# Last attention mixer: all products from tokens in natural order, the dilated order made in the rotation and by a scratch in DRAM

## The chip, the cores and the metric

One core of a Trainium2 chip runs the whole program. The metric is device time in microseconds (us) of one execution, lower is better. A measurement of this kernel has a median over some runs, here three.

## The reference, cut to what matters

The program is a chain of layers on 512 tokens of 1024 features in float32: two hybrid layers, then a pooling mixer and an attention mixer, each with a SwiGLU behind it. The change concerns the attention mixer alone. It has 16 heads of 64, in three groups:

```
ATTN_PATTERNS = ((128, 1), (512, 4), (2048, 16))     # window, dilation; 6, 5 and 5 heads
q = rope(h @ Wq) / 8;  k = rope(h @ Wk);  v = h @ Wv
o_g, lse_g = dilated_window_attention(q, k, v, window, dilation)   # per group
alpha = softmax over groups of (logsumexp over the group's heads of lse - log(heads))
y = concat(3 * alpha_g * o_g) @ w_out
```

With dilation 1 a token attends to its own block of 128 and the one before. With dilation 4, tokens t = 4 l + r of one residue r attend among themselves; this is what the program calls (r, l) order: four blocks of 128 tokens with one residue each. The third group (dilation 16) is computed in the same four blocks with a mask.

## The kernel before, in words

Activations lie feature-major: `h[k]` is a tile [128 features, 2, 512 tokens], high and low part of the normed activation; a float32 product is three matmuls (high x high, high x low, low x high), `mm3`, lines 216 to 221. Weights come as a stream: `wall` holds chunks of eight tiles [128 x 128] in the order of use; SP loads a chunk (L175), ACT rounds it to a high part (L184), DVE takes the low part (L193), two or three chunks ahead of its use (`prep_to`, called from `take`).

Two product forms exist. `prodF` (one weight tile per feature tile, eight of them, 24 matmuls) has the weights as the loaded (stationary) operand and 512 tokens of `h` as the moving one. `prodT` gives token-major results: the loaded operand is a block of 128 tokens of `h`, the moving one is a strip of weight columns; 8 feature tiles x 4 token blocks x 3 = 96 matmuls, of 384, 384 and 256 columns for `v1`, `v2`, `v3`.

In `attn_mixer` (L1274) heads go in eight pairs j. Pairs 0 to 2 use natural token order, 3 to 7 the (r, l) order (head 11, in pair 5, belongs to the third group). Before the change the (r, l) order is made where TensorE reads `h`: `pview` is `h` with tokens in steps of four (16 bytes), used as the moving operand of the ten `prodF` of queries and keys of pairs 3 to 7, and as the loaded operand (`tpview`) of the `prodT` of `v2` and `v3`. The rotation tables exist in both orders (`cc[0]`, `cc[1]`).

The order of work on TensorE is the order of emission: (0,0), (1,0), (0,1), (1,1) in the boundary, then the loop: query product (0,2), `prodT` of `v1`, key product (1,2), (0,3), (1,3), ... (1,7), then `prodT` of `v2` and of `v3`. Here (0,j) is queries and (1,j) keys of pair j. An evacuation `rot` (L1290) is three DVE operations from PSUM (L1293 to L1295) and a Pool addition (L1296); queries then take two ACT passes (L1303, L1304).

Between products, `pump` lets up to two side threads take one stage each. A thread `pair_gen(j)` has the stages scores and exponentials (L1343, L1346, L1347, L1349), transposes (L1376, copies L1377), and output (L1391, L1392); it may start scores when its keys were set one pump before, and output only when the flag of its values is old ("v1", "v2", "v3"). `alpha_gen` waits for all scores, then has a chain of small DVE and ACT operations with two sets of small matmuls (L1428, L1430) and leaves the weights in `den` (L1462). `drain` pumps with no product in between until a flag is set. After that each pair's output is scaled (L1503), transposed (L1510), split in two parts (L1517, L1518 or the helper `split`, L309, L310), and multiplied by `w_out`.

Of the kernel before, what the change touches and what calls it, by code (L numbers as in the profile page):

```python
# [21 lines left out]
NCH = 488  # L22
# [6 lines left out]
# columns of the packed small parameters  # L29
# [11 lines left out]
# columns of the small constants  # L41
# [8 lines left out]
def _shape_constants():  # L50
    f = np.float32
    i = np.arange(128)
    j = np.arange(512)
    cst = np.zeros((128, NCST), f)
    neg = f(-1e30)
    cst[:, 128:256] = np.where(i[None, :] >= i[:, None], f(0), neg)
    cst[:, 0:128] = cst[:, 256:384] = np.where(i[:, None] >= i[None, :], f(0), neg)
    cst[:, 384:512] = np.where((i[:, None] >= i[None, :]) & (i[:, None] % 4 == i[None, :] % 4), f(0), neg)
    cst[:, 512:640] = (i[:, None] > i[None, :]) & (i[:, None] // 64 == i[None, :] // 64)
    for n in range(2):  # L60
        cst[:, 640 + n] = i // 64 == n
    for r in range(4):
        cst[:, 642 + r] = i // 32 == r
        cst[:, 646 + r] = i % 4 == r
    cst[:, 650] = np.where((i // 32) % 2 == 0, 0.125, 0)
    cst[:, 651] = np.where((i // 32) % 2 == 1, 0.125, 0)
    for g, w in enumerate((2, 4, 8, 16)):
        cst[:, 652 + 16 * g:668 + 16 * g] = (f(w) / np.minimum(np.arange(16) + 1, w).astype(f))[None]
    # retention decays per head: within a block of 128 [key, query], of a query since its block's start, of a key to its block's end
    lg = [math.log1p(-2.0 ** (-5.0 - h)) for h in range(4)]  # L70
    cd = np.zeros((128, 2, 4, 128))
    for h in range(4):
        ok = (i[None, :] // 64) >= (i[:, None] // 64)
        cd[:, 0, h] = np.where(ok, np.exp(np.abs(i[None, :] - i[:, None]) * lg[h]), 0) * 128 ** -0.5
        cd[:, 1, h] = np.exp(i * lg[h])[None]
        cst[:, 716 + h] = np.exp((128 - i) * lg[h]) * 128 ** -0.5
    cd = cd.reshape(128, 1024).astype(f)

    def rope_tab(half, nrow):
        inv = f(10000.0) ** (-np.arange(half, dtype=f) / f(half))  # L80
        ang = (np.arange(512, dtype=f)[None, :] * inv.astype(f)[:, None]).astype(f)
        c, s = np.cos(ang).astype(f), np.sin(ang).astype(f)
        n = nrow // half
        C = np.concatenate([c] * n, 0)
        Sg = np.concatenate([s] * (n // 2) + [-s] * (n // 2), 0)
        return C, Sg

    C, Sg = rope_tab(64, 128)
    cr = np.concatenate([C, Sg], 1)
    half = 32  # L90
    inv = f(1.0) / (f(10000.0) ** (np.arange(0, 64, 2, dtype=f) / f(64)))
    ang = (np.arange(512, dtype=f)[None, :] * inv.astype(f)[:, None]).astype(f)
    c, s = np.cos(ang).astype(f), np.sin(ang).astype(f)
    C = np.concatenate([c] * 4, 0)
    Sg = np.concatenate([s, s, -s, -s], 0)
    perm = (4 * np.arange(128)[None, :] + np.arange(4)[:, None]).reshape(-1)
    cd2 = np.concatenate([C, Sg, C[:, perm], Sg[:, perm]], 1)
    cr2 = np.zeros((128, 8, 128), f)
    for r in range(4):
        for l in range(128):  # L100
            cr2[4 * (l % 32) + r, r, l] = 1
    for ib in range(4):
        for t in range(128):
            cr2[32 * ib + t // 4, 4 + ib, t] = 1
    return dict(cst=cst, cd=cd, cr=cr, cd2=cd2.astype(f), cr2=cr2.reshape(128, 1024))


def emit(tc, A, log, stop=None, dump=None):
# [36 lines left out]
    # ---------------- constants and parameters  # L145
# [18 lines left out]
    # ---------------- the stream of weight tiles  # L164
# [32 lines left out]
    def take(spec):  # L197
        """the next weight tile [128 x 128]; spec = (name, index, first row, column ranges)"""
        i = st["pos"]
        st["pos"] += 1  # L200
        log.append(spec)
        c, o = divmod(i, 8)
        prep_to(c + st["la"])
        h, l = prepped[c]
        for old in [q for q in prepped if q < c - 5]:
            del prepped[old]
        return (h, l, o * 128)
# [15 lines left out]
    # ---------------- side threads  # L223
# [3 lines left out]
    class Flags(dict):  # L227
# [3 lines left out]
        def old(self, *es):  # L231
            """all set, and not since the last pump"""
            return all(e in self and self[e] < tick[0] for e in es)

    def pump(n=2, ada=True):
        """one stage each of up to n side threads, and one of the modulation's"""
# [23 lines left out]
    # ---------------- products  # L260
# [9 lines left out]
    def prodT(name, idx, c0, ncol, view, evac):  # L270
        """token-major product: out[tb] [128 tokens, ncol]; c0: first column, or the column ranges of each tile"""
# [19 lines left out]
    # ---------------- statistics  # L291
    def colsum(out, sq, c0, n):
        """out[:, i] = sum over partitions of columns c0 + 128 i.. of sq"""
# [9 lines left out]
    def bcast(ps, r, n):  # L303
        """columns of r [128 tokens, n] over all partitions: ps[:, token]"""
# [7 lines left out]
    # ---------------- residual, normed activations  # L312
# [27 lines left out]
    def norm_gen(c0, c1, psB, Ac, Bc):  # L340
        """all feature tiles, one a step, each DVE pass behind the next tile's first"""
# [32 lines left out]
    def upd_sq(upd):  # L374
        """x update of a whole tile, its squares added to the running sum"""
# [11 lines left out]
    def boundary(name, idx, nk, k0, xs, upd, norm, cons):  # L387
        """last two m-tiles of a product in token halves, the norm, and the first four tiles of the next product"""
# [15 lines left out]
        def tot(a):  # L404
            """all squares of the half but the last tile's, then with it"""
# [80 lines left out]
    # ---------------- adaptive modulation  # L486
# [68 lines left out]
    # ================= block 1  # L555
    def silu2_evac(dst):
        """twice the silu of a product"""
# [17 lines left out]
    def attention1(l, group1):  # L575
        """group1(cons) runs the norm and the first group of products"""
# [23 lines left out]
        # derived columns  # L600
# [9 lines left out]
        # ---- retention  # L610
# [16 lines left out]
        def attend(po, blocks, vt, hd):  # L627
            """po [dv, 512] += v^T A over key blocks; blocks[jb] = A[jb] [128 keys, 512-128*jb]"""
# [11 lines left out]
        def norm_out(key, hd, po, gcol, sil):  # L640
            """po [tokens, 4 blocks, 128]: gated, normed branch output in hi and lo parts"""
# [58 lines left out]
        # ---- gated linear attention and forget gates  # L700
# [117 lines left out]
        # ---- gates and the branches' products  # L818
# [35 lines left out]
        # ---- forgetting attention  # L854
# [103 lines left out]
        # ---- output product, first four tiles as the mixed tiles come  # L958
# [15 lines left out]
    def ffn(first, up_spec, evac_a, evac_b, down, upd, nxt):  # L974
        """first(cons) runs the norm and the first four tiles; up_spec(which, f, k); evac_a -> temp; evac_b(temp) -> product"""
# [68 lines left out]
    # ---------------- start: modulation, norm and first group, tile by tile  # L1044
    def start_group(cons):
# [27 lines left out]
        def ada_mul(k, nd):  # L1073
            """products of the rows' blocks of shift and scale of feature tile k from the nd-th on, summed on Pool"""
# [11 lines left out]
        def ada_sum(k):  # L1086
            """the other blocks on DVE, a step each, then the whole sum"""
# [9 lines left out]
        def ada_cols(k, fill=iter(())):  # L1097
            """their columns, steps of other sums in between"""
# [14 lines left out]
        def ada_pe(p, k, kks):  # L1113
            """shift and scale of feature tile k as a row"""
# [75 lines left out]
    # ================= block 2  # L1190
# [84 lines left out]
    def attn_mixer(first):  # L1275
# [14 lines left out]
        def rot(ps, j, dst=None):  # L1290
            C, Sg = [cc[0 if j < 3 else 1][:, i] for i in range(2)]
            a, b = t2("ra"), t2("rb")
            V.tensor_tensor(a, ps, C, op=ALU.mult)  # L1293
            V.tensor_tensor(b[0:64], ps[64:128], Sg[64:128], op=ALU.mult)
            V.tensor_tensor(b[64:128], ps[0:64], Sg[0:64], op=ALU.mult)  # L1295
            PL.tensor_tensor(a if dst is None else dst, a, b, op=ALU.add)  # L1296
            return a
# [21 lines left out]
        def scores_exp(j, u):  # L1319
            """scores and their exponentials of one head, [queries, blocks of keys]"""  # L1320
# [31 lines left out]
        def pair_gen(j):  # L1352
            """one pair of heads: scores to unscaled outputs [queries, heads]"""
# [49 lines left out]
        def alpha_gen():  # L1403
            """weights of the three groups per token, times 3 / denominator, left in den"""
# [26 lines left out]
            # ly: all three in (l, r) order, lx: in token order; [128, 3, 4]  # L1431
# [34 lines left out]
        def pview(k, j):  # L1466
            v = lambda i: h[k][:, i].rearrange("p (l r) -> p r l", r=4)
            return v(0), v(1)

# [8 lines left out]
        hp = [pview(k, 0) for k in range(8)]  # L1478
# [4 lines left out]
        tpview = lambda k, tb: (hp[k][0][:, tb], hp[k][1][:, tb])  # L1483
        for which, j in seq[4:]:
            f = (q_evac if which == 0 else k_evac)(j)
            prodF(*W, 0, 8, hs if j < 3 else hp, lambda m, ps: f(ps), c0=qkcols(which, j))
            if (which, j) == (0, 2):
                F.add("go")
                prodT(*W, [cols(2048 + 128 * i) for i in range(3)] + [()], 384, tview, lambda tb, ps: ACT.copy(v1[tb // 2][:, tb % 2, 0:384], ps))
                F.add("v1")  # L1490
        prodT(*W, [cols(2432 + 128 * i) for i in range(3)] + [()], 384, tpview, lambda tb, ps: ACT.copy(v2[tb // 2][:, tb % 2, 0:384], ps))
        F.add("v2")
        prodT(*W, 2816, 256, tpview, lambda tb, ps: ACT.copy(v3[:, tb], ps))
# [121 lines left out]
def _pack(inputs, log):  # L1615
    """the weight tiles in the order of their use, eight to a chunk"""
# [93 lines left out]
```

## Time and profile before

| What | Value |
|---|---|
| Median of 3 runs | 2961.01 us (2960.27 to 2964.32) |
| Profiled execution: span from the first to the last instruction | 2960.5 us |
| TensorE (PE) busy in the span | 2920.0 us, 99% |
| DVE, ACT, POOL busy | 1477.7, 991.8, 442.6 us |
| Start of (0,2), start of the first product with `w_out` | 2304.07, 2533.20 us |
| Chain that ended last: all other engines than PE | 0% |
| End of the last key product (1,7) | 2477.97 us |
| Start of the next product after those of the first four `w_out` columns | 2558.14 us |

The profiled execution has no other time of its own than its span; the median of the runs is 0.5 us above it. PE is matmul, PEld weight load, DVE VectorE, ACT ScalarE, POOL GpSimd, SP the queue that loads weights. Ends of matmuls are modelled, so the distance from start to start of two matmuls tells what one costs. A float32 matmul with a small operand (scores, transposes, outputs) shows as two records.

### The profile page before, as it was taken

The page shows a single profiled execution, that of the slowest core. Times are in us where ns is not written, and L with a number is a line of the kernel's source. Part 1 is how long each engine was busy: PE and PEld are TensorE (multiplying, and loading weights), DVE is VectorE, ACT ScalarE, POOL GpSimd, SP SyncE. Part 2 cuts the span into 40 slices and gives each one's busy share as a digit, 9 for nine tenths or more (in the row PEclk, how much of TensorE's full clock was granted, in tenths as well). Part 3 has the DMA queues.
Part 4 walks back from the last instruction along what each step waited for, and adds up shares of the span by engine and source line. Part 5 has one row for each costly group of instructions (what it writes and reads, how often), then busy time and mean ns, then how long its engine had stood idle before and what let it go on. Part 6 is the DMA issues. An engine that isn't in the chain of part 4 may idle for free. (4 is left out here: it accounts for less than half of the span.)

```text
span 2960.5 us, 35393 instructions
## 1 busy us (share of the span) xinstructions
PE 2920.0 (99%) x14426; PEld 2430.7 (82%) x14426; DVE 1477.7 (50%) x2076; ACT 991.8 (34%) x1510; POOL 442.6 (15%) x301
## 2 busy tenths in 40 slices
PE   7999999999999999999999999999999999999998
PEld 4888878888889888878988889888888757888887
DVE  6867565675445544354543345643334544443233
ACT  4243332332233144333332333432123324333122
POOL 4212010110111222110110112110011100111011
PEclk8999999999999999999999999999999999999999
DMA  7445434444323223223323322322323111322321
GB/s 285 154 152 181 154 114 142 150 143 161 109 90 114 83 85 101 86 72 102 105 86 102 98 93 79 121 79 93 107 86 121 58 37 49 97 88 91 109 86 50
DMA packets 90055, 319.08 MB, mean 108 GB/s; under 512 B 9850, under 2 KB 12060, under 8 KB 89892
## 3 DMA queue, kind: packets, MB, share of 16 engines
q1 hardware_dynamic: 87908, 313.92, 33.1%
q10 hardware_dynamic: 1984, 2.90, 0.3%
q8 instruction: 113, 1.85, 0.3%
q14 instruction: 50, 0.41, 0.0%
HBM read 314.67 MB, written 2.11 MB: 107 GB/s over the span
## 5 line engine op out<-in xcount | busy, mean ns | idle before, releaser
L219 PE MATMUL mm<-h,wh 128*128 128x512 f32 (+1 forms) x2424 | 930.9, 384 | 0.0
L221 PE MATMUL mm<-h,wl 128*128 128x512 f32 (+1 forms) x2424 | 924.8, 381 | 0.3 <-DVE wl L193 0.3
L220 PE MATMUL mm<-h,wh 128*128 128x512 f32 (+1 forms) x2424 | 925.1, 382 | 0.0
L193 DVE TENSOR_TENSOR wl<-w,wh 128x1024 fp32r<-128x1024 f32 x483 | 630.7, 1312 | 50.6 <-ACT wh L184 49.0
L184 ACT CAST wh<-w 128x1024 fp32r<-128x1024 f32 x488 | 502.1, 1046 | 184.6 <-DVE wl L193 76.6
L221 PEld LDWEIGHTS mm<-h,wl 128*128 128x128 f32 x2424 | 459.0, 189 | 97.8 <-issue 20.2
L219 PEld LDWEIGHTS mm<-h,wh 128*128 128x128 f32 x2424 | 459.0, 189 | 94.7 <-issue 18.7
L220 PEld LDWEIGHTS mm<-h,wh 128*128 128x128 f32 x2424 | 459.1, 189 | 93.5 <-issue 17.7
L219 PE MATMUL mm<-y,wh 128*128 128x512 f32 (+1 forms) x704 | 264.6, 376 | 0.0
L220 PE MATMUL mm<-y,wh 128*128 128x512 f32 (+1 forms) x704 | 264.6, 376 | 0.0
L221 PE MATMUL mm<-y,wl 128*128 128x512 f32 (+1 forms) x704 | 264.5, 376 | 0.0
L282 PE MATMUL mm<-wh,h 128*128 128x512 f32 (+3 forms) x480 | 182.4, 380 | 0.5 <-DVE rb L1295 0.5
L284 PE MATMUL mm<-wl,h 128*128 128x512 f32 (+3 forms) x480 | 179.5, 374 | 0.0
L283 PE MATMUL mm<-wh,h 128*128 128x512 f32 (+3 forms) x480 | 179.3, 374 | 0.0
L981 DVE TENSOR_TENSOR g<-g,mm 128x512 f32<-128x512 f32 x44 | 30.3, 688 | 285.2 <-PE mm L221 276.4
L219 PEld LDWEIGHTS mm<-y,wh 128*128 128x128 f32 x704 | 132.5, 188 | 24.2
L220 PEld LDWEIGHTS mm<-y,wh 128*128 128x128 f32 x704 | 132.5, 188 | 24.1
L221 PEld LDWEIGHTS mm<-y,wl 128*128 128x128 f32 x704 | 132.5, 188 | 24.0
L310 POOL TENSOR_TENSOR y<-u,y 128x512 fp32r<-128x512 f32 x44 | 68.2, 1550 | 525.2 <-ACT y L309 515.9
L310 POOL TENSOR_TENSOR y<-g,y 128x512 fp32r<-128x512 f32 x44 | 68.1, 1547 | 522.7 <-ACT y L309 522.7
L523 DVE SCALAR_TENSOR_TENSOR adaacc<-ada,cact,adaacc 128x512 f32<-128x512 f32 x140 | 127.3, 910 | 3.0
L384 POOL TENSOR_TENSOR acc<-acc,sq 128x512 f32<-128x512 f32 x40 | 59.5, 1486 | 460.0 <-ACT sq L383 459.4
(372 smaller groups left out, 3381.3 us busy)
## 6 DMA issues: line engine op xcount, KB each, us to landing
w<-in_wall SPq DMA_DIRECT2D x488, 512.0 KB, 3.6
ada<-in_wada SPq DMA_DIRECT2D x96, 512.0 KB, 3.6
x<-in_xT SPq DMA_DIRECT2D x8, 256.0 KB, 6.3
cB<-scr ACTq DMA_DIRECT2D x8, 256.0 KB, 4.2
cR<-in_cr SPq DMA_DIRECT2D x2, 512.0 KB
cD<-in_cd SPq DMA_DIRECT2D x2, 512.0 KB, 5.7
c<-in_cd SPq DMA_DIRECT2D x2, 512.0 KB
out<-out SPq DMA_DIRECT2D x2, 512.0 KB, 3.1
```

The source lines that it names most:

```text
L184: ACT.copy(his[i], stage[i])
L193: (eng or V).tensor_tensor(l, stage.pop(i), his[i].bitcast(F32), op=ALU.subtract)
L219: PE.matmul(ps, wh, xh, start=start, stop=False)
L220: PE.matmul(ps, wh, xl, start=False, stop=False)
L221: PE.matmul(ps, wl, xh, start=False, stop=stop)
L282: PE.matmul(ps[tb][:, 0:ncol], xh, wh, start=k == 0, stop=False)
L283: PE.matmul(ps[tb][:, 0:ncol], xl, wh, start=False, stop=False)
L284: PE.matmul(ps[tb][:, 0:ncol], xh, wl, start=False, stop=k == 7)
L310: (eng or V).tensor_tensor(hl[:, 1], src, hl[:, 0].bitcast(F32), op=ALU.subtract)
L384: PL.tensor_tensor(sqa["acc"], sqa["acc"], q, op=ALU.add)
L523: V.scalar_tensor_tensor(acc, src, cact[:, kk:kk + 1], acc, op0=ALU.mult, op1=ALU.add)
L981: V.tensor_tensor(s, s, ps, op=ALU.mult)
```

## The change

Queries and keys of all pairs are now multiplied from `h` in natural order. For pairs 3 to 7 `rot` reads PSUM with a step of four elements and writes in (r, l) order. The values come from two `prodT` of 512 columns instead of three of 384, 384 and 256: the first gives `v1` and the first 128 columns of `v2`, the second the rest. What belongs to `v2` and `v3` is copied by ACT to temporary tiles, written to a DRAM scratch [512, 640] by DMAs from the ACT queue (four of 64 KB, four of 256 KB), and read back in (r, l) order by three DMAs of the same queue. The second `prodT` moves from the end of the loop to behind the key product (1,2). The flags "v2" and "v3" are both set after the loop. The stream has 486 chunks instead of 488.

```diff
         def rot(ps, j, dst=None):
             C, Sg = [cc[0 if j < 3 else 1][:, i] for i in range(2)]
             a, b = t2("ra"), t2("rb")
-            V.tensor_tensor(a, ps, C, op=ALU.mult)
-            V.tensor_tensor(b[0:64], ps[64:128], Sg[64:128], op=ALU.mult)
-            V.tensor_tensor(b[64:128], ps[0:64], Sg[0:64], op=ALU.mult)
+            if j < 3:
+                v = lambda t: t
+            else:
+                v = lambda t: t.rearrange("p (r l) -> p r l", r=4)
+                ps = ps.rearrange("p (l r) -> p r l", r=4)
+            V.tensor_tensor(v(a), ps, v(C), op=ALU.mult)
+            V.tensor_tensor(v(b[0:64]), ps[64:128], v(Sg[64:128]), op=ALU.mult)
+            V.tensor_tensor(v(b[64:128]), ps[0:64], v(Sg[0:64]), op=ALU.mult)
             PL.tensor_tensor(a if dst is None else dst, a, b, op=ALU.add)
...
+        scr2 = dr.tile([S, 640], F32, name="scr2")
+        vperm = scr2.rearrange("(l r) c -> l r c", r=4)
+        def v_evac(tb, ps):
+            ACT.copy(v1[tb // 2][:, tb % 2, 0:384], ps[:, 0:384])
+            t = t2("vs")
+            ACT.copy(t[:, 0:128], ps[:, 384:512])
+            nc.scalar.dma_start(scr2[tb * 128:(tb + 1) * 128, 0:128], t[:, 0:128])
+        def w_evac(tb, ps):
+            t = t2("vs")
+            ACT.copy(t, ps)
+            nc.scalar.dma_start(scr2[tb * 128:(tb + 1) * 128, 128:640], t)
         for which, j in seq[4:]:
             f = (q_evac if which == 0 else k_evac)(j)
-            prodF(*W, 0, 8, hs if j < 3 else hp, lambda m, ps: f(ps), c0=qkcols(which, j))
+            prodF(*W, 0, 8, hs, lambda m, ps: f(ps), c0=qkcols(which, j))
             if (which, j) == (0, 2):
                 F.add("go")
-                prodT(*W, [cols(2048 + 128 * i) for i in range(3)] + [()], 384, tview, lambda tb, ps: ACT.copy(v1[tb // 2][:, tb % 2, 0:384], ps))
+                prodT(*W, 2048, 512, tview, v_evac)
                 F.add("v1")
-        prodT(*W, [cols(2432 + 128 * i) for i in range(3)] + [()], 384, tpview, lambda tb, ps: ACT.copy(v2[tb // 2][:, tb % 2, 0:384], ps))
+            if (which, j) == (1, 2):
+                prodT(*W, 2560, 512, tview, w_evac)
+                for i in range(2):
+                    nc.scalar.dma_start(v2[i][:, :, 0:384], vperm[:, 2 * i:2 * i + 2, 0:384])
+                nc.scalar.dma_start(v3, vperm[:, :, 384:640])
         F.add("v2")
-        prodT(*W, 2816, 256, tpview, lambda tb, ps: ACT.copy(v3[:, tb], ps))
         F.add("v3")
```

## Rows read from the trace of the kernel before

**Rows 1.** Page of the profile, busy time of each engine.
```profile
PE 2920.0 (99%) x14426; PEld 2430.7 (82%) x14426; DVE 1477.7 (50%) x2076; ACT 991.8 (34%) x1510; POOL 442.6 (15%) x301
```

**Rows 2.** Timeline, PE, product (0,2), natural order: start us, us, engine, line, operation.
```profile
2306.13 0.39 PE L219 MATMUL mm<-h,wh 128*128 128x512 f32 x1
2306.36 0.39 PE L220 MATMUL mm<-h,wh 128*128 128x512 f32 x1
```

**Rows 3.** Timeline, PE: start of product (1,4), and of what follows its 24 matmuls.
```profile
2387.08 0.70 PE L219 MATMUL mm<-h,wh 128*128 128x512 f32 x1
...
2398.21 0.84 PE L1328 MATMUL sd<-k,q 128*128 128x128 f32 x4
```

**Rows 4.** Timeline, PE, the token-major products of `v1`, then of `v3`.
```profile
2313.10 0.33 PE L283 MATMUL mm<-wh,h 128*128 128x384 f32 x1
2313.27 0.33 PE L284 MATMUL mm<-wl,h 128*128 128x384 f32 x1
...
2515.05 0.40 PE L282 MATMUL mm<-wh,h 128*128 128x256 f32 x1
2515.29 0.40 PE L283 MATMUL mm<-wh,h 128*128 128x256 f32 x1
```

**Rows 5.** Groups of weight loads in 2309 to 2334, then 2492 to 2530: busy us, mean ns.
```profile
L283 PEld LDWEIGHTS mm<-wh,h 128*128 128x128 f32 x32 | 6.0, 188 | 0.1
...
L283 PEld LDWEIGHTS mm<-wh,h 128*128 128x128 f32 x48 | 15.8, 330 | 0.0
```

**Rows 6.** Timeline, all engines, last key product's rotation and the last pair's scores.
```profile
2478.19 0.69 DVE L1293 TENSOR_TENSOR ra<-mm,c 128x512 f32<-128x512 f32 x1 [6.80 <-PE mm L221]
2480.42 1.29 POOL L1296 TENSOR_TENSOR k<-ra,rb 128x512 f32<-128x512 f32 x1 [11.47 <-DVE rb L1295]
2484.53 1.95 PE L1343 MATMUL sd<-k,q 128*128 128x128 f32 x16
2485.69 0.69 DVE L1346 TENSOR_TENSOR e<-sd,cst 128x512 f32<-128x512 f32 x1 [2.90 <-PE sd L1343]
2487.14 0.41 ACT L1349 ACTIVATE e<-e,nmx 128x128 f32<-128x128 f32 x1 [6.54 <-DVE nmx L1347]
2490.25 1.03 ACT L184 CAST wh<-w 128x1024 fp32r<-128x1024 f32 x1
```

**Rows 7.** Three source lines: ns min/median/max; L1518 writes and reads in steps of four elements.
```profile
L309 ACT CAST o<-sd x3: 592/594/608, 2532.6 to 2538.9; 128x512 fp32r<-128x512 f32 x3
...
L1518 DVE TENSOR_TENSOR o<-sd,o x5: 1085/1091/1096, 2546.8 to 2559.6; 128x512 fp32r<-128x512 f32 x5
...
L310 DVE TENSOR_TENSOR o<-sd,o x3: 684/691/693, 2533.2 to 2539.6; 128x512 fp32r<-128x512 f32 x3
```

**Rows 8.** Timeline, the weights of the groups (`alpha_gen`), then one pair's output.
```profile
2493.66 1.28 ACT L1409 ACT_TABLE_LOAD   x1
2499.93 0.31 DVE L1423 TENSOR_SCALAR lg<-lg 128x4 f32<-128x4 f32 x3
2504.12 0.95 PE L1428 MATMUL sd<-lg,pm 128*128 128x4 f32 x8
2506.53 0.16 DVE L1444 TENSOR_SCALAR lx<-lg 128x4 f32<-128x4 f32 x1
2507.74 0.16 DVE L1451 TENSOR_REDUCE m<-lx 128x4 f32<-128x12 f32 x1
2511.01 0.36 DVE L1462 TENSOR_TENSOR den<-den,q 128x24 f32<-128x24 f32 x3
2536.53 1.89 PE L1391 MATMUL sd<-v,pt 128*128 128x64 f32 x16
```

**Rows 9.** Timeline, ACT queue in layer 0: a DRAM scratch written, then read by four DMAs.
```profile
228.67 0.53 ACTq L740 DMA_DIRECT2D scr<-fp  x1
230.11 1.90 ACTq L742 DMA_DIRECT2D cB<-scr  x4
```

**Rows 10.** Windows: us, busy of PE, PEld, DVE, ACT, POOL, granted clock, DMA share, GB/s.
```profile
1866.00:1870.00 4.00, 4.00 (x13) 3.12 (x13) 2.50 (x6) 1.31 (x2) 0.00 (x0) 0.65 0.19 20
```

More of the change, by code (lines that the diff above doesn't have):

```diff
@@ L21 @@
 EPS = 1e-6
-NCH = 488
+NCH = 486
 LA, LD = 2, 1
@@ L1464, in alpha_gen @@
             yield
-        def pview(k, j):
-            v = lambda i: h[k][:, i].rearrange("p (l r) -> p r l", r=4)
-            return v(0), v(1)
         seq = []
@@ L1477, in attn_mixer @@
         hs = hx()
-        hp = [pview(k, 0) for k in range(8)]
         v1 = [g4("v1", shape=(128, 2, 512)) for _ in range(2)]
@@ L1482, in attn_mixer @@
         tview = lambda k, tb: (h[k][:, 0, tb * 128:(tb + 1) * 128], h[k][:, 1, tb * 128:(tb + 1) * 128])
-        tpview = lambda k, tb: (hp[k][0][:, tb], hp[k][1][:, tb])
+        scr2 = dr.tile([S, 640], F32, name="scr2")
[9 more added lines that the diff above has]
+            nc.scalar.dma_start(scr2[tb * 128:(tb + 1) * 128, 128:640], t)
         for which, j in seq[4:]:
             f = (q_evac if which == 0 else k_evac)(j)
-            prodF(*W, 0, 8, hs if j < 3 else hp, lambda m, ps: f(ps), c0=qkcols(which, j))
+            prodF(*W, 0, 8, hs, lambda m, ps: f(ps), c0=qkcols(which, j))
             if (which, j) == (0, 2):
                 F.add("go")
-                prodT(*W, [cols(2048 + 128 * i) for i in range(3)] + [()], 384, tview, lambda tb, ps: ACT.copy(v1[tb // 2][:, tb % 2, 0:384], ps))
+                prodT(*W, 2048, 512, tview, v_evac)
                 F.add("v1")
-        prodT(*W, [cols(2432 + 128 * i) for i in range(3)] + [()], 384, tpview, lambda tb, ps: ACT.copy(v2[tb // 2][:, tb % 2, 0:384], ps))
+            if (which, j) == (1, 2):
[3 more added lines that the diff above has]
+                nc.scalar.dma_start(v3, vperm[:, :, 384:640])
         F.add("v2")
-        prodT(*W, 2816, 256, tpview, lambda tb, ps: ACT.copy(v3[:, tb], ps))
         F.add("v3")
```

## The prediction

> **What bounds the kernel now.** I read the page's busy times first: TensorE is busy for 99% of the span [rows 1], and the chain of waits names no other engine. So time can only come from TensorE's own work in the stretch that is changed, and can be lost there only where TensorE is made to wait. That stretch is (0,2) to the first product with `w_out`, 2304.07 to 2533.20, 229 us. In its timeline I looked at the distance from start to start of two matmuls. With tokens in natural order 512 columns cost 0.23 us [rows 2]; I use 0.227, the 24 of a product 5.45 us. In the ten products of pairs 3 to 7, whose moving operand is read in steps of 16 bytes, 24 matmuls take 11.13 us [rows 3], 0.464 each, with nothing else on TensorE between. In the token-major products 384 columns cost 0.173 for `v1`, but 0.233 for `v2` and also for `v3`, which has only 256 columns [rows 4]. There the loaded operand is read in steps: the weight load takes 330 ns instead of 188 [rows 5], and the load, not the columns, sets the pace.
>
> **The change part by part**, against the span of 2960.5 us.
>
> *Ten products become contiguous.* 10 x (11.13 - 5.45) = -56.8 us.
>
> *Values.* Before, the three products took 17.7 us (`v1`, with 1.1 us of stalls; the work is 96 x 0.173), 22.9 and 22.5 (about 96 x 0.233 each), together 63.1. After, 2 x 96 x 0.227 = 43.6: -19.5 us. Two weight chunks fewer to prepare lie beside TensorE: nothing.
>
> *Side work on TensorE* (scores, transposes, outputs) is the same and stays on the path: 0. What changes is how well it is covered, since the products between are half as long.
>
> *The rotation reads PSUM in steps of four.* No row shows that. Low end: no dearer, 0.69 us an operation [rows 6]. Nearest row: a DVE operation from PSUM with an SBUF output and one input in steps of four, 1.09 against 0.69 [rows 7]. High end: twice 0.69, 1.38, as a moving operand in steps doubled on TensorE [rows 2, 3]. I take 1.09, from the same engine. DVE is idle over half of the span [rows 1], so the price comes only through latency, as follows.
>
> *Stalls before transposes.* Let t = 0 be the end of product (0,j+1), when scores of pair j start. DVE first has the rotation of these queries: from 0.22 (2477.97 to 2478.19, [rows 6]) for 3 x 1.1 to 3.55. Then two additions and two reductions of 0.69 each; the first maximum is there at 4.95. ACT is in order: the queries' two passes of 0.72 come first (Pool's addition takes 1.3, so they end at 6.45), then eight exponentials in 3.1 us (2487.14 to 2490.25, [rows 6]): 9.6. TensorE has done scores (1.7 from their start to what follows, here and below) and product (1,j+1) (5.45) at 7.15, transposes the first head and waits for the second's exponentials: it ends at 10.05 instead of 7.95, a stall of 2.1 us. Before, the product of 11.13 covered this. For pairs 3, 4, 5: +6.3 (0.9 each, 2.7, at the low end; 2.9 each, 8.7, at the high end). Pair 6 falls into the next part. Scores themselves do not wait: keys are ready at 5 us, the product in between is 5.45 and transposes 0.8.
>
> *The tail.* Before, the products of `v2` and `v3` lay behind (1,7) and covered the last pair's scores and the whole chain of `alpha_gen`. After, nothing is left but side work. From the end of (1,7), t = 0: pair 6's transposes end at 2.9; keys of pair 7 are ready at 0.22 + 3.3 + 1.3 = 5.0 (with the wait for Pool); scores start; their exponentials end 5.7 later (2484.53 to 2490.25, [rows 6]), 10.8. The outputs of pairs 3 to 6 fill TensorE from 6.7 to 13.7 (1.73 each, [rows 8]); each one's copy waits on ACT behind those exponentials, then pair 7's transposes and copies follow, to 15.2. Only then comes the first table load of `alpha_gen` on ACT: its first part takes 6.6 us (2493.66 to 2500.24), the second 2.6 (2504.12 to 2506.69), the third 3.6 (2507.74 to 2511.37) [rows 8]: 28.1. Scaling, transposes and the first half of the split (0.69 and 0.59, [rows 7], with 0.4 of matmuls and hand-overs) bring the first `w_out` product to 30.0. TensorE's own work in it (transposes twice 0.8, scores 1.7, five outputs 8.65, the small matmuls 1.7, transposes for `w_out` 0.7) is 14.4; idle 15.6, of which 0.5 were there before: +15.1. Low end, with a rotation of 2.1: 14; high end 16.5.
>
> *Scratch.* ACT gets eight copies more or other, eleven DMA issues of about 0.45 (four in 1.90, [rows 9]), and the reads wait for the last write to land: 1.4 us between write and read in the earlier scratch [rows 9], of 8 KB only. Behind the waiting read on ACT stand the next weight cast, pair 2's last copy and queries (0,3). The second product's copies and issues end at 4.3 us, pair 2's exponentials at 6.4, the reads are issued by 8 to 10, and nothing of that is needed by TensorE before 13 (pair 2's outputs, after (1,3)); casts run three chunks ahead. Price 0, and 5 us if the write takes 10 us to land. Readers of `v2` and `v3` come 90 us later. The first product's evacuation delays pair 0's and 1's exponentials by 2 us: +0.5. SP's queue sees only the faster use of chunks, the pace that the feed-forward layers have all along.
>
> *Clock.* Behind a pause of TensorE in the pooling mixer the granted clock was 0.65 of full over 4 us [rows 10], 2.8 us at the lower of its two levels (1.2 GHz), which lost 1.4 us of work. The change makes new pauses, about 5 us twice in the tail and 2 us before each pair's transposes. I count three or four such dips, +5 us; bounds 0 and 10.
>
> Sum: -56.8 - 19.5 + 6.3 + 15.1 + 0.5 + 5 = -49.4. 2960.5 - 49.4 = 2911.1 for the span, and 0.5 more for the median: 2911.6.
>
> **Rivals.**
> *A, steps in PSUM cost nothing and the clock stays up:* -56.8 - 19.5 + 2.7 + 14 + 0.5 = -59, 2902. For it: PSUM is not SBUF, where the rows show the price. Against: DVE paid 0.4 us more for such steps.
> *B, the rotation costs twice:* stalls 8.7, tail 16.5, clock 8: -42.6, 2918. The Trainium skill bears on this (PSUM - Partial Sum Buffer, Specifications): it gives PSUM lines of 8 bytes and says that any non-contiguous access slows matmuls significantly; for DVE's reads it gives no figure and no run here shows one.
> *C, the products stay at 11.13 us, as steps are not what makes them slow:* only the values are won, -19.5, and the tail lost, +15 and clock +2: 2959. For it: the modelled ends say nothing of a cause. Against: (0,2) and (1,4) differ in the view of `h` alone, and the loads show the same [rows 2, 3, 5]. The Trainium skill (SBUF - State Buffer, "Door 1: The DMA port swizzle") would speak for C: it says that four float32 are a step that one can take for free. The trace disagrees: exactly that step takes 0.464 instead of 0.227.
> *D, slower than before:* DVE becomes the bound of pairs 3 to 7. Per pair it has six rotation operations of X, 2.4 us of weight preparation and 3.4 of scores and copies, 6X + 5.9; before, a pair took 24.8 us of TensorE. Values and tail together are about even, so it decides at 6X + 5.9 > 24.8: X = 3.2 us, 4.6 times the contiguous one. At X = 3.5 it is 5 x 2.1 and a tail longer by 3 x 2.8: some 2975. Against: the dearest step in these rows is 2.05 times.
>
> **How the numbers follow.** The forecast, 2911.6, with its terms between their bounds: 0.60. A 0.17, B 0.13, C 0.03, D 0.02, and 0.05 for a stall that I did not see, above 2926 (the write that lands late, or chunks that come late). The range 2896 to 2926 takes in A and B with some room and leaves about 0.2 outside. About 0.2% is what a measurement of this kernel can tell from no change, 6 us: faster 0.95, same 0.03, slower 0.02.
>
> **What would show it.** Right: matmuls of pairs 3 to 7 at 0.227 us; 192 instead of 288 token-major ones, all at 0.227; between the end of (1,7) and the first `w_out` product about 30 us with TensorE half idle; L1376 waiting some 2 us for exponentials; rotation operations of pairs 3 to 7 at 1.09 us, the term that I know least. Wrong: a wait of TensorE on weights (L193) or of ACT on the scratch's reads over 5 us, a tail far from 30 us, or products of pairs 3 to 7 over 6 us.

## The result and the profile after

The changed kernel takes 2905.95 us, median of 4 runs (2904.25 to 2915.56), against 2962.49 for the kernel before in the same comparison: ratio 0.9817, 95% interval 0.9801 to 0.9832. Forecast were 2911.6 us and a range of 2896 to 2926. The profiled execution has a span of 2904.6 us, 55.9 less than before; the stretch from the start of (0,2) to the last 24 matmuls of the first four `w_out` columns (2303.84 to 2502.20, against 2304.07 to 2558.14) is shorter by 55.7 of them, so next to nothing happened elsewhere. The table of the kernel before calls 2558.14 the start of the product behind those columns; in the trace it is the start of these 24 matmuls. The longest of the four runs, 2915.56 us, is the one with the lowest mean granted clock, 0.989 against 0.993 and 0.994.

The page's busy row, which answers to [rows 1]; TensorE has 68 us less to do:

```profile
PE 2852.1 (98%) x14330; PEld 2402.7 (83%) x14330; DVE 1477.6 (51%) x2074; ACT 989.9 (34%) x1508; POOL 442.0 (15%) x301
```

The timeline of TensorE, changed kernel: two neighbouring matmuls of the second token-major product (they answer to [rows 4]), then the start of query product (0,6) and of what follows it (to [rows 3]). 24 matmuls now take 5.58 us instead of 11.13, and the token-major matmuls of 512 columns are 0.23 us apart:

```profile
2366.89 0.39 PE L283 MATMUL mm<-wh,h 128*128 128x512 f32 x1
2367.12 0.40 PE L284 MATMUL mm<-wl,h 128*128 128x512 f32 x1
...
2421.92 0.49 PE L219 MATMUL mm<-h,wh 128*128 128x512 f32 x1
...
2427.50 0.38 PE L1349 MATMUL sd<-k,q 128*128 128x128 f32 x2
```

The first operation of the rotation by its source line, ns min/median/max. Six of the 16 read PSUM contiguously and ten in steps of four, and all take the same. So the step has no price here; I had taken 1.09 us from [rows 7]:

```profile
L1299 DVE TENSOR_TENSOR ra<-mm,c x16: 684/692/692, 2303.0 to 2449.0; 128x512 f32<-128x512 f32 x16
```

The timeline of all engines from the end of (0,7) to the first `w_out` product; (1,7) ends at 2448.76. The chain to follow: rotation, exponentials (to the weight cast at 2449.77), transposes that wait a moment for them, then scores of pair 7 that wait for the keys, the table load on ACT, the small matmuls, the group weights, the transposes for `w_out`. It answers to [rows 6, 8]:

```profile
2441.78 0.69 DVE L1299 TENSOR_TENSOR ra<-mm,c 128x512 f32<-128x512 f32 x1 [2.22 <-PE mm L221]
2446.68 0.39 ACT L1355 ACTIVATE e<-e,nmx 128x128 f32<-128x128 f32 x1
2449.77 1.03 ACT L184 CAST wh<-w 128x1024 fp32r<-128x1024 f32 x1
...
2448.76 1.48 PE L1382 MATMUL sd<-ident,e 128*128 128x128 f32 x8
2452.89 2.05 PE L1349 MATMUL sd<-k,q 128*128 128x128 f32 x16 [2.65 <-POOL k L1302]
...
2463.55 1.28 ACT L1415 ACT_TABLE_LOAD   x1
2470.09 1.84 PE L1434 MATMUL sd<-lg,pm 128*128 128x4 f32 x8 [4.77 <-issue]
2477.69 0.36 DVE L1468 TENSOR_TENSOR den<-den,q 128x24 f32<-128x24 f32 x3
2478.82 1.94 PE L1528 MATMUL sd<-ident,os 128*128 128x128 f32 x8 [5.17 <-DVE os L1521]
2480.58 0.80 PE L219 MATMUL mm<-o,wh 128*128 128x512 f32 x1
```

From the end of (1,7) to the first `w_out` product 31.8 us pass, which I call the tail; forecast were 30.0 and something for the clock. The waits of TensorE's matmuls from 2380 to 2500 (us in total, times, longest) are these four and no others:

```profile
PE sd L1528 <- DVE os L1521: 5.2, 1, 5.2
PE sd L1434 <- issue: 4.8, 1, 4.8
PE sd L1349 <- POOL k L1302: 2.6, 1, 2.6
PE sd L1397 <- DVE pt L1383: 0.4, 1, 0.4
```

Windows of the tail, with busy times of PE, PEld, DVE, ACT, POOL, then granted clock, DMA share and GB/s (they answer to [rows 10]). The clock goes to its lower level, 1.2 GHz, at 2468.3 and stays there for 17.1 us; the small matmuls are 0.21 us apart instead of 0.11, and the first 12 `w_out` matmuls take 5.2 us instead of 3.3:

```profile
2460.00:2468.00 8.00, 4.88 (x43) 4.54 (x41) 1.85 (x8) 4.77 (x7) 0.00 (x0) 1.00 0.34 118
2468.00:2480.60 12.60, 5.33 (x25) 5.08 (x25) 5.96 (x33) 4.32 (x8) 0.00 (x0) 0.51 0.04 8
2480.60:2485.80 5.20, 5.20 (x14) 3.76 (x14) 3.58 (x5) 1.53 (x2) 0.00 (x0) 0.55 0.26 93
```

The scratch, by the DMA view (KB each, median us to landing). The first read is issued at 2384.58, 5.1 us behind the last write's issue, and ACT was idle for 3.43 us before the weight cast behind the reads; TensorE waits for nothing there. It answers to [rows 9]:

```profile
v<-scr ACTq DMA_DIRECT2D x1, 512.0 KB, 6.3
...
scr<-vs ACTq DMA_DIRECT2D x4, 256.0 KB, 2.0
```

### The profile page after: what moved, and what is told of

Read it like the earlier page. It is cut to its first block, busy times and chain, and to the rows that moved or that the text cites. A ratio compares the mean times of both kernels' runs of the same rounds, so it can differ in the third digit from the quotient of the medians.

```text
span 2904.6 us, 35206 instructions
## 1 busy us (share of the span) xinstructions
PE 2852.1 (98%) x14330; PEld 2402.7 (83%) x14330; DVE 1477.6 (51%) x2074; ACT 989.9 (34%) x1508; POOL 442.0 (15%) x301
## 4 chain that ended last, share of the span: by engine, by line
PE 94%; DVE 3%; ACT 1%; issue 1%; POOL 1%; DMA 0%; SPq 0%; DVEq 0%; POOLq 0%; ACTq 0%
PE mm L219 25%; PE mm L220 25%; PE mm L221 25%; PE mm L282 3%; PE mm L284 3%; PE mm L283 3%; PE sd L219 1%; PE sd L220 1%; PE sd L221 1%; PE sd L630 1%; PE sd L904 1%; PE sd L296 0%; POOL rs L301 0%; DVE wl L193 0%; DVE ab L1092 0%
## 5 line engine op out<-in xcount | busy, mean ns | idle before, releaser
L219 PE MATMUL mm<-h,wh 128*128 128x512 f32 (+1 forms) x2424 | 909.5, 375 | 0.0
L220 PE MATMUL mm<-h,wh 128*128 128x512 f32 (+1 forms) x2424 | 903.5, 373 | 0.0
L221 PE MATMUL mm<-h,wl 128*128 128x512 f32 (+1 forms) x2424 | 902.9, 372 | 0.3 <-DVE wl L193 0.3
L282 PE MATMUL mm<-wh,h 128*128 128x512 f32 (+1 forms) x448 | 171.1, 382 | 0.1
L284 PE MATMUL mm<-wl,h 128*128 128x512 f32 (+1 forms) x448 | 168.2, 375 | 0.0
L283 PE MATMUL mm<-wh,h 128*128 128x512 f32 (+1 forms) x448 | 168.1, 375 | 0.0
```

What stands on the lines that cost most here:

```text
L219: PE.matmul(ps, wh, xh, start=start, stop=False)
L220: PE.matmul(ps, wh, xl, start=False, stop=False)
L221: PE.matmul(ps, wl, xh, start=False, stop=stop)
L282: PE.matmul(ps[tb][:, 0:ncol], xh, wh, start=k == 0, stop=False)
L283: PE.matmul(ps[tb][:, 0:ncol], xl, wh, start=False, stop=False)
L284: PE.matmul(ps[tb][:, 0:ncol], xh, wl, start=False, stop=k == 7)
```

## The experiments

| Kernel | us, median | Ratio to before, 95% |
|---|---|---|
| the change | 2905.95 | 0.9817 (0.9801 to 0.9832) |
| the change, measured again (`e10`) | 2908.65 | 0.9821 (0.9807 to 0.9834) |
| rotation alone (`e1`) | 2907.36 | 0.9814 (0.9799 to 0.9829) |
| values alone (`e2`) | 2969.46 | 1.0019 (1.0009 to 1.0029) |
| values alone, pauses filled (`e9`) | 2958.91 | 0.9987 (0.9978 to 0.9996) |
| the change, pauses filled (`e7`) | 2903.37 | 0.9802 (0.9788 to 0.9816) |
| the change, group weights' thread first (`e6`) | 2909.18 | 0.9825 (0.9811 to 0.9839) |
| the change, second values product last (`e4`) | 2896.37 | 0.9776 (0.9761 to 0.9790) |
| `e4` with the scratch read by SP (`e8`) | 2891.16 | 0.9761 (0.9747 to 0.9774) |
| before, in steps of two (`e5`) | 2942.38, one run | - |

The theory: the ten contiguous products give 56 us; what the values give, 18 us, is lost again in the tail that their products used to cover, part of it by the clock. The rivals: the values have a gain of their own; the tail is bound by DVE and ACT alone; the scratch's round trip is the price.

**e1, the rotation alone.** The values as before:

```diff
-                prodT(*W, 2048, 512, tview, v_evac)
+                prodT(*W, [cols(2048 + 128 * i) for i in range(3)] + [()], 384, tview, ...)
...
+        prodT(*W, [cols(2432 + 128 * i) for i in range(3)] + [()], 384, tpview, ...)   # behind the loop
+        prodT(*W, 2816, 256, tpview, lambda tb, ps: ACT.copy(v3[:, tb], ps))
```

> Half of the change alone: the ten query and key products of pairs 3 to 7 read h in natural order and the rotation permutes; the values are as before (three token-major products, those of v2 and v3 at the end of the loop, from tokens in steps). My theory: the products give -55.7 us and two things hang on the values alone, -18.3 us of work and the uncovered tail, +17 and +2 for the clock, which cancel. So 2962.5 - 55.7 + 1.5 of stalls before transposes = 2908 us, as fast as the whole change (2906); no pause over 1 us between (1,7) and the first w_out product, and the granted clock stays up there. Rival: the values carry a gain of their own and the tail's pause was there anyway: then 2925 us.

2907.36 us, as forecast, and not to be told from the whole change. All that TensorE waited for from 2420 to 2485 was half a microsecond:

```profile
PE mm L219 <- ACT o L309: 0.3, 1, 0.3
PE mm L220 <- DVE o L310: 0.2, 1, 0.2
```

The granted clock was at its lower level for 3.4 us some 28 us behind the end of (1,7), and in the kernel before for as long 29 us behind it. So the whole gain is the rotation's, and the tail's pauses come from the moved values.

**e2, the values alone.** The products of pairs 3 to 7 take `h` in steps again, and the rotation is as before:

```diff
...
-            prodF(*W, 0, 8, hs, lambda m, ps: f(ps), c0=qkcols(which, j))
+            prodF(*W, 0, 8, hs if j < 3 else hp, lambda m, ps: f(ps), c0=qkcols(which, j))
```

> The other half alone: values by two contiguous token-major products and the DRAM scratch, the second one behind (1,2); the products of pairs 3 to 7 read h in steps as before, the rotation is as before. My theory: -18.3 us for the products of the values, +17 in the tail and +2 for the clock there: 2963 us, the same as before (2962.5), with L1376 not waiting for exponentials and the first w_out product 31 to 32 us behind the end of (1,7). Rival: the scratch and the moved product are worth their 18 us, the tail is a matter of the shorter products: 2944 us.

2969.46 us: dearer than I expected, a miss of 6 us on the side of my theory. The tail takes 40.9 us (2501.94 to 2542.79) instead of 31.8. Its windows show what differs: the clock goes down at 2504.8, in the first pause, and stays down for 41 us, so that outputs and transposes run at the lower level too:

```profile
2501.90:2510.00 8.10, 5.01 (x28) 4.73 (x26) 4.22 (x7) 0.87 (x2) 1.26 (x1) 0.68 0.01 3
2510.00:2530.00 20.00, 18.77 (x87) 18.21 (x87) 3.14 (x10) 8.76 (x24) 0.00 (x0) 0.50 0.08 28
2530.00:2542.80 12.80, 5.33 (x25) 5.07 (x25) 5.93 (x33) 4.52 (x9) 0.00 (x0) 0.50 0.15 44
```

**e7, the change with filled pauses.**

```diff
+        def fill(n):
+            d = mmb()
+            for i in range(n):
+                PE.matmul(d, h[i % 8][:, 0, 0:128], h[i % 8][:, 0], start=i == 0, stop=i == n - 1)
...
+        fill(10)      # behind the loop, ahead of the drain; fill(18) ahead of py, px; fill(20) behind them
```

> The whole change, with matmuls of no use in the three pauses of the tail (10 while the last keys are rotated, 18 ahead of the small matmuls, 20 behind them; 512 columns each into a spare PSUM tile, 11 us in all). It takes no wait away and adds work. My theory, the fall of the granted clock costs 4 us of the tail: the clock stays up, the small matmuls go from 0.213 to 0.112 us, the first w_out product from 5.2 to 3.3 us, time 2906 - 4 = 2902. Rival: the tail is bound by DVE and ACT alone and the clock costs nothing: 2906, or more where the useless matmuls run into the useful ones.

2903.37 us. In the trace the tail is 29.8 us instead of 31.8 and the first 12 `w_out` matmuls take 3.4 instead of 5.2, 3.9 us together: the forecast size. The whole trace is only 2.5 us shorter, because (1,7) ends 1.5 us later in it (2450.22 instead of 2448.76). By the medians the gain is 2.6 and 5.3 us against the two measurements of the change. Their eight runs reach from 2904.25 to 2915.56 us, those of this kernel from 2903.12 to 2903.88, under all of them, though the intervals of the ratios overlap. Work of no use made the kernel faster, so the clock, and not only DVE and ACT, is part of the tail. The window of the tail:

```profile
2460.00:2480.00 20.00, 18.38 (x119) 15.58 (x118) 7.80 (x41) 10.38 (x19) 0.00 (x0) 1.00 0.15 54
```

**e9, the values alone with filled pauses, and e10.** The three `fill` of e7 in the kernel of e2; and the changed kernel once more.

> e2_values_only with the useless matmuls of e7_filled_pauses in the same three pauses. e2 came out at 2969.5, 7.5 us over the kernel before, where I had 2963; its granted clock was down from the first pause of the tail on, for 41 us, and the tail took 40.9 us instead of 31.8. My theory, the excess is the clock and nothing of the scratch or the products: with the clock held up the tail is the 29.8 us of e7, the first w_out product takes 3.4 us, and the time is 2962 - 18.3 + 15.4 - 0.5 = 2958. Rival: the excess lies elsewhere (longer products, the scratch), and the time stays above 2964.

> The changed kernel as it is, on the same chip and in the same rounds as e9: 2906 us, against which e7's 2903.4 and e8's 2891.2 are to be read. If a part of their lead were the chip's, this would come out near 2903.

2958.91 us, where 2958 were expected: with the clock up the tail takes 29.8 us (2505.24 to 2535.01), the values alone are worth 4 us, and e2's excess was the clock; the intervals of e2 and e9 lie apart. The scratch and the longer products are in both kernels, so they are not behind it. Two of e2's own ten runs say the same: with a mean granted clock of 0.994 and 0.992 they took 2959.49 and 2963.17 us, while the other eight, at 0.989 and 0.990, took 2967.7 to 2970.6. e10 gave 2908.65. It ran on the chip of e9, while e7 and e8 ran on another; the kernel before took 2962.76 us on the first and 2961.56 on the second, so some 1.2 us of the leads of e7 and e8 over e10 (5.3 and 17.5 us) may be the chip's, and the rest is the kernels'. The window of e9:

```profile
2501.00:2533.00 32.00, 30.18 (x186) 24.75 (x184) 12.03 (x47) 13.90 (x33) 1.27 (x1) 1.00 0.13 41
```

**e6, the group weights' thread first.** In the change its first table load stands on ACT behind the copies of four outputs and of pair 7's transposes; here the thread comes first and yields between its parts:

```diff
-        side.extend(pair_gen(j) for j in range(8))
         side.append(alpha_gen())
+        side.extend(pair_gen(j) for j in range(8))
...
+            yield
             ACT.activation(tmp, tmp, AF.Exp)
...
+            yield
             lg = c16("lg")
...
+            yield
             yield
             yield
             py, px = sdb(), sdb()
```

> The whole change, but the thread of the groups' weights stands ahead of the pairs and yields between its three ACT parts, so that its first table load comes right behind the last pair's exponentials instead of behind the copies of four outputs and of pair 7's transposes; work and products are the same. My theory, ACT's order is a link of the tail: the first table load 4 to 5 us earlier against the end of (1,7), the first w_out product at 28 us behind it instead of 31.8, time 2906 - 4 = 2902. Rival: the copies come late instead, outputs of pairs 5 and 6 wait for PSUM, and the time stays at 2906.

2909.18 us, no gain: the rival's time held, and its reason is a part of it. The table load did come 4.7 us earlier (10.1 us behind the end of (1,7) at 2448.91, instead of 14.8), and the small matmuls 3.3 us. But outputs and transposes now waited for copies on ACT, as the waits of TensorE show:

```profile
PE sd L1382 <- ACT oT L1398: 0.9, 1, 0.9
PE sd L1397 <- ACT oT L1398: 0.6, 1, 0.6
```

The rest of the lead was given back behind the small matmuls: the last output ran behind them, at the lower clock (it fell at 2461.6, 6.7 us earlier), its copy stood in front of the next table load on ACT, and the exponentials behind that load came no earlier than in the change. Timeline of ACT; the first row is the early load, the others the place where the lead was lost:

```profile
2458.96 1.28 ACT L1415 ACT_TABLE_LOAD   x1
...
2473.86 0.58 ACT L1398 COPY oT<-sd 128x512 f32<-128x512 f32 x1 [6.13 <-PE sd L1397]
2474.47 1.28 ACT L1462 ACT_TABLE_LOAD   x1
```

**e4 and e8, the second values product last.** e4 moves it behind (1,7), with side threads in it; the first three pairs' `w_out` products cover the scratch. e8 lets SP issue the reads, right behind the product:

```diff
...
-            if (which, j) == (1, 2):
-                prodT(*W, 2560, 512, tview, w_evac)
...
+        prodT(*W, 2560, 512, tview, w_evac, at=(1, 3, 5, 6))   # pumps behind these k, and one ahead of the evacuation
...
-        for j in range(8):
+        for j in range(3): scale_o(j)
+        for j in range(3): trans_o(j)
+        for i in range(2):
+            nc.scalar.dma_start(v2[i][:, :, 0:384], vperm[:, 2 * i:2 * i + 2, 0:384])   # e8: nc.sync, behind prodT
+        nc.scalar.dma_start(v3, vperm[:, :, 384:640])
+        F.add("v2")
+        F.add("v3")
+        wo(0, range(4))
+        wo(1, range(4))
+        scale_o(3)
+        scale_o(4)
+        trans_o(3)
+        wo(2, range(4))
+        for j in range(3, 8):
...
```

> The whole change, but the second product of the values comes last, behind (1,7), with side threads at four places in it, so that it covers the last pair's scores, transposes and the weights of the groups; the reads of the scratch follow, and the w_out products of pairs 0 to 2 cover them. My theory: the pause of the tail and the fall of the clock go: -15 us, 2892 us, first w_out product some 32 us behind (1,7) with the 22 us product in it, granted clock up, and a pause of some 5 us left where ACT evacuates before the first split. Rival: the round trip through DRAM becomes the new wait in front of the outputs of pairs 3 and 4 (over 8 us), and the time stays at 2902 to 2906.

> As e4_values_last, but the three reads of the scratch are issued by SP right behind the product's evacuation instead of by ACT behind the splits. In e4 ACT stood 4.6 us in front of these reads with a weight cast behind it, and the outputs of pair 3 waited 1.8 us for them, after which the clock fell. My theory: reads land 3 us earlier, no wait for them, no fall of the clock at that place: 2896 - 4 = 2892. Rival: SP's weight chunks now stand behind the reads and come late, 2896 or more.

e4: 2896.37 us, 10 to 12 us under the change where 15 were expected. Of the tail's 13 us of pauses 2.3 are left, in front of the first transposes for `w_out`. But ACT stood idle in front of the reads and the outputs of pair 3 waited for them, as the rival had it, with a smaller price, and the clock, which was to stay up, fell behind these waits. Waits of e4, ACT's and TensorE's, and the window with the fall:

```profile
ACT wh L184 <- issue: 4.6, 1, 4.6
...
PE sd L1399 <- DMA v<-scr: 1.8, 2, 1.1
...
2467.30:2478.30 11.00, 10.22 (x48) 9.33 (x49) 3.64 (x4) 3.12 (x4) 0.00 (x0) 0.69 0.35 105
```

e8: 2891.16 us, the time as forecast. TensorE does not wait for SP's chunks or for the reads, and at the outputs of pair 3 the clock stays up. It did fall elsewhere, for 3.4 us from 2459.2 on, behind the 2.3 us in which TensorE waits for ACT; behind the same pause of 2.3 us in e4 it did not fall. It is the fastest version, 2.4% under the kernel before and 0.5 to 0.6% under the change. What TensorE still waits for in it, from 2420 to 2500, and the window with the fall:

```profile
PE sd L1527 <- ACT vs L1498: 2.3, 1, 2.3
PE mm L219 <- ACT o L311: 0.2, 1, 0.2
...
2457.50:2466.80 9.30, 9.07 (x37) 6.81 (x38) 4.11 (x6) 3.13 (x6) 0.00 (x0) 0.82 0.73 247
```

**e5, the kernel before in steps of two.**

```diff
-            v = lambda i: h[k][:, i].rearrange("p (l r) -> p r l", r=4)
+            v = lambda i: h[k][:, i].rearrange("p (l r) -> p r l", r=2)
...
-        tpview = lambda k, tb: (hp[k][0][:, tb], hp[k][1][:, tb])
+        tpview = lambda k, tb: tuple(hp[k][i][:, tb // 2, tb % 2 * 128:tb % 2 * 128 + 128] for i in range(2))
```

> The kernel before, but where it reads h in steps of four elements (16 bytes) it reads it in steps of two (8 bytes), for the moving operand of the ten products and for the loaded one of v2 and v3; it leaves out the (r, l) order, so its tokens are mixed up in pairs 3 to 7. Question: what makes a step dear? Theory 1, two values per 16 bytes are enough for full speed: 0.227 us per matmul, loads at 188 ns, time 2962.5 - 56 - 16 = 2890 us. Theory 2, any step costs the same: 0.464 and 330 ns, 2962 us. Theory 3, the price grows with the bytes passed over: about 0.34 us and 260 ns, 2930 us.

2942.38 us, a single run, and no theory alone holds. The moving operand costs nearly the same at 8 bytes as at 16: 0.452 and 0.464 us a matmul. The loaded one does not: 195 ns instead of 330, and the 256-column matmuls take 0.12 us instead of 0.233, so it was the load that had set their pace. The products of `v2` and `v3` take 28.6 us instead of 45.4, which with some 2.9 us for the ten products (240 matmuls) makes up the 19.6 us gained. Timeline of TensorE in a query product and in the product of `v3`:

```profile
2446.40 0.63 PE L219 MATMUL mm<-h,wh 128*128 128x512 f32 x1
2446.85 0.63 PE L220 MATMUL mm<-h,wh 128*128 128x512 f32 x1
...
2500.05 0.28 PE L282 MATMUL mm<-wh,h 128*128 128x256 f32 x1
2500.17 0.28 PE L283 MATMUL mm<-wh,h 128*128 128x256 f32 x1
```

and a group of its weight loads (busy us, mean ns), to be set beside [rows 5]:

```profile
L283 PEld LDWEIGHTS mm<-wh,h 128*128 128x128 f32 x64 | 12.5, 195 | 0.0
```

## Why the prediction was right, and which terms were off

| Step | Forecast, us | Measured, us | From |
|---|---|---|---|
| ten products contiguous | -56.8 | -55.7 | 24 matmuls take 5.54 to 5.68 with the hand-over; all ten products 55.7 against 111.4 |
| values' products | -19.5 | -18.3 | 44.8 against 63.1 |
| stalls before transposes | +6.3 | +1.1 | transposes of pairs 3 to 5 take 1.16 to 1.19 instead of 0.80 |
| tail without the clock | +15.1 | +14.9 | e7: 29.8, less TensorE's own work as forecast (14.4) and 0.5 of before |
| clock | +5 | +3.9 | change against e7: tail 2.1, first `w_out` product 1.8 |
| evacuation of the first product | +0.5 | -0.9 | the scores of the first two heads in the first values product take 3.24 instead of 4.15 |
| sum | -49.4 | -55.0 | span: -55.9 |

The mechanism was right and so was each sign but the smallest. The mis-sized term is the stall before the transposes: forecast 2.1 us a pair, measured 0.38. It failed first with its premise, the price of a DVE operation that reads PSUM in steps, for which I took 1.09 us from an operation that writes and reads SBUF in steps; it is 0.69. With that the eight exponentials end 8.3 us behind the scores' start (2441.51 to 2449.77) and not 9.6. The low bound of the same working had the price right and still gave 0.9 a pair. The rest is a second step: I let all four transposes of the second head wait for its last exponential. In the trace of the changed kernel the transposes run as the exponentials come, and only one weight load of a pair's eight waits for one, 0.25 us. Timeline of TensorE (PE) and its weight loads (PEld), pair 5:

```profile
2434.74 1.43 PE L1382 MATMUL sd<-ident,e 128*128 128x128 f32 x8
2435.84 0.14 PEld L1382 LDWEIGHTS sd<-ident,e 128*128 128x128 f32 x1 [0.25 <-ACT e L1355]
2435.93 0.49 PE L219 MATMUL mm<-h,wh 128*128 128x512 f32 x1
```

Of the 6.5 us between forecast and span the stalls make 5.2. The evacuation (1.4), the clock (1.1) and the tail (0.2) go the same way, the misses of the two groups of products (1.1 and 1.2) the other; 0.9 us are not put down to anything.

Two terms came out nearer than their working, which is luck. For the clock I counted three or four dips of 1.4 us, some of them before the transposes of single pairs; there was one fall, of 17.1 us, and none before the tail. For the tail I used the dear rotation: the scores of pair 7 start 4.1 us behind (1,7) instead of 5.0 and their exponentials end at 9.9 instead of 10.8, but by the table load only 0.4 us of this is left (14.8 instead of 15.2).

Rival A had the rotation right; its time of 2902 was too low because the clock did fall, and with the clock held up e7 takes 2903.4. The first measurement, 2905.95, lies nearer to A than to the forecast, the second, 2908.65, nearer to the forecast. Rival B's doubled rotation did not happen: DVE's reads take 692 ns in both forms. The rule of the Trainium skill on PSUM's lines (PSUM - Partial Sum Buffer, Specifications) speaks of matmuls, and this trace shows that it does not carry over to these reads. Rival C, in which steps are not what makes the products slow, fell at once: the matmuls are 0.23 us apart. Rival D never came near its deciding point of 3.2 us.

What I did not see beforehand is how little the second half of the change brings. The sum had it (-19.5 against +15.1 and +5), but the text did not say that the two halves could be had apart. e1 and e2 show that the rotation alone gives the whole gain and that the values alone lose; e9 shows that they win 4 us when the clock stays up.

## What to carry to other kernels

Look at the distance from start to start of matmuls and ask for each stretch whether the moving operand, the loaded one or the columns set it: an operand in steps can double a matmul while TensorE shows as busy. Move a permutation to an engine with slack, and test the price of its access there instead of taking it from another memory. When a product is moved away from the end of a stage, what it covered must get another cover: last in the order goes the work on which the chain does not depend (e4, e8).

## What the runs showed of the hardware that I had not expected

- A matmul with 512 columns of `h` as the moving operand (four bytes an element) costs 0.227 us contiguous, 0.452 in steps of 8 bytes (e5) and 0.464 in steps of 16. The load of 128x128 of `h` takes 188 ns contiguous, 195 in steps of 8 and 330 in steps of 16. The Trainium skill (SBUF - State Buffer, "Door 1: The DMA port swizzle") says that two hits per 16-byte line suffice for full bandwidth; the loads agree with that, the moving operand does not.
- DVE reads PSUM in steps of 16 bytes at the contiguous price (692 ns for 512 columns), while with SBUF on the strided side it took 1.09 us [rows 7].
- A fall of the granted clock can last far longer than the pause in which it came. In e2 it came in a pause of 3.1 us and lasted 41 us, through 20 us in which TensorE was busy for 18.8 with small matmuls; in the change it came in the pause behind the outputs and lasted 17.1 us; with matmuls of 512 columns in the pauses (e7, e9) it did not come in the tail at all.
